# Reading the expert tiles in a circle that the token blocks join one by one, and comparing both keys in one VectorE operation for three of four tables

## The chip, the cores and the metric

The kernel runs on one core of a Trainium2 chip. The metric is the device time of one launch in microseconds (us); the time of the kernel before is the median of three runs. The engines are named as in the profile: PE (TensorE matmul; PEld its weight loads), DVE (VectorE), ACT (ScalarE), POOL (GpSimd) and SP (SyncE). SP issues plain DMAs, POOL issues gathers (indirect DMAs).

## What is computed

One layer of a transformer over 128 context tokens and 512 latent tokens of width 1024: adaptive norms, retention heads and neighbourhood attention, an output projection, and then PEER, a retrieval over 16384 single-neuron experts. The change is in PEER alone. For a block of 128 tokens, cut from the reference:

```
v1, i1 = top_k(s1, 16);  v2, i2 = top_k(s2, 16)        # 8 heads, two sets of 128 keys
top, sel = top_k(v1[:, None] + v2[None, :], 16)         # 16 of 256 pairs
eidx = i1 * 128 + i2  (of sel);   gate = softmax(top)
act = gelu(einsum('nd,nhkd->nhk', xb, u[eidx]))
y   = einsum('nhk,nhkd->nd', gate * act, v[eidx])
```

Each token has 128 chosen experts (8 heads of 16). `u` and `v` have 16384 rows of 1024 floats. There are five blocks of 128 tokens.

## The kernel before, in words

**Two ways through PEER.** For all five blocks, the rows of `u` are gathered: 128 gathers a block, each of 128 rows of 4 KB, one chosen expert for every token. DVE takes the dot product of each gathered tile with the block's input (a SCALAR_TENSOR_TENSOR of 128x1024). The fifth block, block 4, gathers its rows of `v` in the same way and adds them up in PSUM. Blocks 0 to 3 instead read all of `v`: they build a table W of weights, token by expert, and multiply it with `v`, read as 128 tiles of 128 rows (512 KB each). Tile i holds the experts with first key i.

**The tables.** `Dense.build(b)` (line 1571) builds the table of block b in 64 pairs of tokens. For a token it makes two one-hot matrices over the token's 128 chosen experts: one of the first key, scaled by the weight, and one of the second key. Their product, on PE, is the token's 128x128 table, second key by first key. For a pair m, DVE compares a row of numbers with the first keys (line 1600, bf16 result `eq`) and with the second keys (line 1601, fp32 result `B_`); ACT scales `eq` into `A_`, once for each token (line 1606); PE multiplies (two tokens); and every second pair ACT copies four tokens' tables from PSUM to `W` (line 1608). `eqs` and `oneh` have two buffers each, used in turn; `tabs`, which hold the keys and weights of the block, are one set.

There is room for two tables, `W[0]` and `W[1]`. Blocks 0 and 1 are group g = 0, blocks 2 and 3 group g = 1; block b uses `W[b % 2]`. Group 0 lays the table out so that the product's step i uses the memory rows i, and group 1 lays it out turned, so that token n lies in row n. So a token's table of block 2 can be written as soon as step n of block 0's product is done; each product needs its whole table.

**The products.** `product(0)` (line 1620) reads tile by tile of v and does four 128x512 matmuls with each, two for block 0 and two for block 1, in four PSUM banks. `product(1)` does the same for blocks 2 and 3. The last five tiles of the first round are kept and used first in the second (`NKEEP`), so v is read 251 times. `Stream` (line 444) holds the tiles of v in flight: a quota of six of the six tiles of the ring. `self.at` counts the steps done, and `build` of group 1 waits for it (line 1597). At the end of a product, `finish` (line 1551) closes a block in four pieces of 256 columns through one ring tile, halves of it in turn; `finish_with` (line 1543) closes a block from tiles loaded before.

**What sets the order.** The functions above are generators that record operations; `main` and `gathers` are interleaved by a count of PE and DMA time. `build(0)` is recorded beside the last key scores (line 1325); then `dense` (line 1678) records `build(1)`, then `product(0)` beside `build(2)` and `build(3)` (these two with PSUM banks 4 and 5 only), then `product(1)`. A planner (class `Plan`, from line 111) then orders all operations by their data, their priority and prices of its own (`cost`, lines 192 to 215), several times over, and emits the order that it finds shortest. Each engine runs its instructions in that order. Everything recorded passes line 365, so the profile names that line for all; the tile names tell the groups apart: `w` is the ring (and v), `arena` holds tables, gather tiles and the rest, `iota` marks the tables' compares. The gathers use tiles of their own (`gslots`, two at first, eight or nine late in the span).

Of the kernel before, what the change touches and what calls it, by code (L numbers as in the profile page):

```python
# [29 lines left out]
ROUNDS = ((0,), (1, 2, 3))  # L30
AHEADU = 1
XTRA = 3
NKEEP = 5


def bcast_rows(ap, n, width, offset=0):
# [332 lines left out]
def layer(ctx: ExitStack, tc: tile.TileContext, a: dict):  # L369
# [46 lines left out]
    def within(lo, hi, g):  # L416

        while True:
            old, banks[:] = list(banks), (lo, hi)
            r = next(g, "end")  # L420
            banks[:] = old
            if r == "end":
                return
            yield r

    def mm(out, lhsT, rhs, start, stop):
        nc.tensor.matmul(out, lhsT=lhsT, rhs=rhs, start=start, stop=stop)
        k, m = lhsT.shape[0], int(np.prod(lhsT.shape[1:]))
        n = int(np.prod(rhs.shape[1:]))
        up = lambda v: 32 if v <= 32 else 64 if v <= 64 else 128  # L430
        clk["PE"] += 4 * n / 2400.0 * up(k) / 128 * up(m) / 128
# [64 lines left out]
            ar.free(*lent.pop(id(t)))  # L496
            slots[:] = [x for x in slots if x is not t]

    S, SB, SV = Stream(NRING), Stream(2), Stream(NRING)

    def add_w(name, r, j, w, keep=None):
        for qt in range(4):
# [42 lines left out]
    for bl in ROUNDS:  # L545
        for h in range(8):
            lo, hi = 6 - 2 * bl[-1], 14 - 2 * bl[0]
            SB.add(("bias", bl, h), a["bias"][:, h, lo:hi, :], [hi - lo, 64])
    for t in list(range(P)) + list(range(P - NKEEP)):
        SV.add(("v", t), a["v"][P * t:P * t + P], [D])  # L550


    tc.nc.scalar.preload_act_table_set("natural_log_exp_and_others")
# [2 lines left out]
    def reserve():  # L556

        all_ = ar.alloc([19, P], lo=0, hi=12 * 256 // UNIT).ap
        oneh[:] = [all_[:, 4 * i:4 * i + 4].rearrange("s (z n) i -> s z n i", z=2) for i in range(2)]
        eqs[:] = [all_[:, 8 + i].bitcast(BF16).rearrange("s (i n) -> s i n", n=2) for i in range(2)]  # L560
        tabs[:] = [all_[:, 12], all_[:, 13], all_[:, 14].bitcast(BF16).rearrange("s (z n) -> s z n", z=2)]
        scb[:] = [all_[:, 15:19]]
        spare[:] = [all_[:, 0:8].rearrange("s a b -> s (a b)")]
# [974 lines left out]
    def prefetch(b, g, x):  # L1538
        if g is not None:
            nc.sync.dma_start(g, g2d[0 if b == 0 else 1])  # L1540
        nc.sync.dma_start(x, xres[b])

    def finish_with(b, acc, g, x):

        for j in range(2):
            col = slice(512 * j, 512 * j + 512)
            nc.vector.tensor_mul(acc[j], acc[j], g[:, col])
            nc.vector.tensor_add(x[:, col], x[:, col], acc[j])
            nc.sync.dma_start(a["y"][P * b:P * b + P, col], x[:, col])

    def finish(b, acc, t):

        for j in range(4):
            col = slice(256 * j, 256 * j + 256)
            g, x = (t[:, 512 * (j % 2) + 256 * z:512 * (j % 2) + 256 * z + 256] for z in range(2))
            nc.sync.dma_start(g, g2d[0 if b == 0 else 1][:, col])
            nc.sync.dma_start(x, xres[b][:, col])
            nc.vector.tensor_mul(g, acc[j // 2][:, 256 * (j % 2):256 * (j % 2) + 256], g)
            nc.vector.tensor_add(x, x, g)
            nc.sync.dma_start(a["y"][P * b:P * b + P, col], x)  # L1560
# [4 lines left out]
    class Dense:  # L1565
        def __init__(self):
            self.W = [None, None]
            self.at = P
            self.vkeep = {}

        def build(self, b):

            g, q = divmod(b, 2)
            if self.W[q] is None:
                self.W[q] = ar.alloc([P, P], top=True)
            Wn = self.W[q].ap
            if g == 0:
                Wn = Wn.rearrange("j i n -> j n i")
            while (b, 3) not in cready:
                yield "wait"  # L1580

            bt = bank()
            tr(bt.ap[:, 0:P], cw[b].rearrange("q h k -> q (h k)"))
            cT, ti, keys = tabs
            tii = ti.bitcast(I32)
            id_ = idx[b].rearrange("q h k -> q (h k)")
            for z, (op, s) in enumerate(((OP.arith_shift_right, 7), (OP.bitwise_and, 127))):
                nc.vector.tensor_single_scalar(tii, id_, s, op=op)
                nc.vector.tensor_scalar(ti, tii, 1.0, None, op0=OP.mult)
                tr(bt.ap[:, P * (z + 1):P * (z + 2)], ti)  # L1590
            nc.scalar.copy(cT, bt.ap[:, 0:P])
            nc.scalar.copy(keys, bt.ap[:, P:3 * P].rearrange("s (z n) -> s z n", z=2))
            ps.free(bt)
            full = None
            for m in range(P // 2):
                n0 = 2 * m
                while g == 1 and self.at < min(n0 + 4, P) and n0 % 4 == 0:
                    yield "at"
                eq, A_, B_ = eqs[m % 2], oneh[m % 2][:, 0], oneh[m % 2][:, 1]
                nc.vector.tensor_tensor(eq, iota2, keys[:, 0, None, n0:n0 + 2].to_broadcast([P, P, 2]), op=OP.is_equal)  # L1600
                nc.vector.tensor_tensor(B_, iota2.rearrange("s i n -> s n i"),
                                        keys[:, 1, n0:n0 + 2, None].to_broadcast([P, 2, P]), op=OP.is_equal)
                if n0 % 4 == 0:
                    bw = bank()
                for k in range(2):
                    nc.scalar.activation(A_[:, k], eq[:, :, k], AF.Copy, scale=cT[:, n0 + k:n0 + k + 1])
                if full is not None:
                    nc.scalar.copy(*full)
                    ps.free(last)
                    full = None  # L1610
                for k in range(2):
                    z = n0 % 4 + k
                    mm(bw.ap[:, P * z:P * z + P], B_[:, k], A_[:, k], True, True)
                if n0 % 4:
                    full, last = (Wn[:, n0 - 2:n0 + 2, :], bw.ap.rearrange("j (n i) -> j n i", n=4)), bw
                    yield
            nc.scalar.copy(*full)
            ps.free(last)

        def product(self, g):  # L1620
            acc = [[ps.alloc([512], hi=4) for _ in range(2)] for _ in range(2)]
            order = range(P) if g == 0 else list(range(P - NKEEP, P)) + list(range(P - NKEEP))
            for n, i in enumerate(order):
                if i not in self.vkeep:
                    v = SV.get(("v", i))
                else:
                    v = self.vkeep.pop(i)
                for q in range(2):
                    w = self.W[q].ap[:, i, :] if g == 0 else self.W[q].ap[:, :, i]
                    for j in range(2):  # L1630
                        mm(acc[q][j].ap, w, v[:, 512 * j:512 * j + 512], n == 0, n == P - 1)
                if g == 0 and i >= P - NKEEP:
                    self.vkeep[i] = v
                elif g == 0 and i == P - NKEEP - 1:
                    free = SV.held.pop(0)
                else:
                    SV.done()
                self.at = n + 1
                if g == 1 and n == P - 3:
                    last = [slots.pop() for _ in range(3)]  # L1640
                    prefetch(2, last[0], last[1])
                    prefetch(3, None, last[2])
                if n % 2:
                    yield
            while g == 1 and "v4" not in done:
                yield "wait"
            nc.gate = mark[0] if g == 1 else None
            for q in range(2):
                if g == 0:
                    finish(q, [x.ap for x in acc[q]], free)  # L1650
                    if q == 1:
                        slots.append(free)
                        SV.pump()
                else:
                    finish_with(2 + q, [x.ap for x in acc[q]], last[0], last[1 + q])
                ps.free(*acc[q])

    def both(*work):

        live = list(work)  # L1660
        while live:
            w = 0
            for z in list(live):
                r = next(z, "end")
                if r == "end":
                    live.remove(z)
                elif r is not None:
                    w += 1
                else:
                    yield  # L1670
            if live and w == len(live):
                yield "wait"

    def chain(*work):
        for w in work:
            yield from w

    def dense(dn):
        yield from dn.build(1)
        dn.at = 0  # L1680
        yield from both(dn.product(0), within(4, 6, chain(dn.build(2), dn.build(3))))
        yield from dn.product(1)


    def main():
# [127 lines left out]
```

## Time and profile before

| | us |
|---|---|
| three runs: median (lowest to highest) | 1906.23 (1904.07 to 1906.36) |
| the profiled execution, its own time | 1904.95 |
| its span, first to last instruction | 1903.1 |
| PE busy | 1777.2 (93%) |
| DVE busy | 1467.7 (77%) |
| ACT busy | 532.2 (28%) |
| POOL busy | 834.4 (44%) |

DMA moved 658.22 MB, a mean of 346 GB/s; 402.70 MB of it on POOL's queue (the gathers), 254.16 MB on SP's. The granted clock of PE was 0.958 of full speed on average.

How to read it: busy shares are averages over stages in which different resources are full, so the page's slices of 1/40 of the span and windows of chosen stretches say more. PE's busy time is of pipelined matmuls. A group's row has its count, busy time, mean, and the idle time of the engine just before its instructions with what ended it. A 128x512 fp32 matmul shows as two rows, so a tile of v for two blocks is eight.

### The profile page before, as it was taken

How to read it: one execution, taken by the hardware profiler on the slowest of the kernel's cores; microseconds unless marked ns; L12 is line 12 of the kernel's file. 1: busy time of each engine (PE TensorE's matmuls, PEld its weight loads, DVE VectorE, ACT ScalarE, POOL GpSimd, SP SyncE). 2: the span in 40 equal slices, each digit the busy share in tenths (PEclk: the TensorE clock that was granted, in tenths of full speed). 3: DMA queues.
4: the chain of work that ended last, by engine and by line, in shares of the span. 5: the costliest groups of instructions: out<-in, count | busy, mean ns of one | idle time of the engine just before them, and what ended most of it. 6: DMA issues, size and time to landing. Idle time of an engine off the chain costs nothing.

```text
span 1903.1 us, 21175 instructions
## 1 busy us (share of the span) xinstructions
PE 1777.2 (93%) x6096; PEld 1063.2 (56%) x6096; DVE 1467.7 (77%) x3785; ACT 532.2 (28%) x1368; POOL 834.4 (44%) x779
## 2 busy tenths in 40 slices
PE   7999999999999889867999999899987999999997
PEld 2438454455965466555444444355665666666665
DVE  2246998786879999999999996777998566666666
ACT  1225320133434334698211110122674000000000
POOL 0000467542137666524555544444435344444442
PEclk9998999999979889977999999899997999999999
DMA  9997889988759999857999999999978999999998
GB/s 363 316 327 246 313 278 339 393 311 307 271 178 344 365 336 378 317 177 210 364 408 401 392 408 409 387 409 406 358 242 275 410 409 409 409 409 409 409 409 330
DMA packets 203693, 658.22 MB, mean 346 GB/s; under 512 B 22572, under 2 KB 25900, under 8 KB 203448
## 3 DMA queue, kind: packets, MB, share of 16 engines
q0 software_dynamic: 110592, 402.70, 56.7%
q1 hardware_dynamic: 92984, 254.16, 35.5%
q8 instruction: 49, 0.80, 0.2%
q14 instruction: 68, 0.56, 0.1%
HBM read 645.51 MB, written 11.27 MB: 345 GB/s over the span
## 4 chain that ended last, share of the span: by engine, by line
DMA 27%; DVE 18%; PE 12%; issue 6%; ACT 2%; POOL 1%; DVEq 0%; POOLq 0%; ACTq 0%
DMA arena<-in_u,idx 15%; PE psum L365 12%; DMA arena<-in_v,idx 12%; DVE arena L365 12%; ACT arena L365 2%; DVE psum L365 1%; POOL arena L365 1%; DVE i L365 1%; DVE oh L365 1%; DVE vi L365 1%; DVE cand L365 0%; DVE idx L365 0%; DVE pi L365 0%; DMA w<-xres 0%; DMA out_y<-w 0%
## 5 line engine op out<-in xcount | busy, mean ns | idle before, releaser
L365 PE MATMUL psum<-w,arena 128*128 128x512 f32 (+1 forms) x2548 | 1094.2, 600 | 17.4 <-DVE arena L365 6.5
L365 POOL DMA_INDIRECT arena<-in_u,idx x640 | 711.6, 1112 | 899.8 <-DVE arena L365 486.6
L365 PEld LDWEIGHTS psum<-w,arena 128*128 128x128 f32 (+1 forms) x2548 | 560.4, 229 | 456.3 <-issue 280.2
L365 PE MATMUL psum<-arena 128*128 128x128 f32 (+5 forms) x2532 | 543.4, 366 | 65.3 <-ACT arena L365 34.1
L365 PEld LDWEIGHTS psum<-arena 128*128 128x128 f32 (+2 forms) x2532 | 374.3, 206 | 273.8 <-issue 137.3
L365 DVE SCALAR_TENSOR_TENSOR arena<-arena 128x1024 f32<-128x1024 f32 (+5 forms) x451 | 488.7, 1091 | 27.6 <-DMA arena<-in_u,idx 25.0
L365 DVE SCALAR_TENSOR_TENSOR arena<-arena,psum 128x1024 f32<-128x1024 f32 x256 | 308.4, 1214 | 92.6 <-DMA arena<-in_u,idx 92.6
L365 ACT ACTIVATE arena<-arena 128x128 f32<-128x128 bf16 (+7 forms) x626 | 237.7, 433 | 224.4 <-PE psum L365 103.8
L365 ACT COPY arena<-psum 128x512 f32<-128x512 f32 (+3 forms) x360 | 204.0, 581 | 316.6 <-PE psum L365 287.0
L365 DVE SCALAR_TENSOR_TENSOR psum<-arena,cw,psum 128x1024 f32<-128x1024 f32 x127 | 163.7, 1289 | 96.1 <-DMA arena<-in_v,idx 96.0
L365 DVE TENSOR_TENSOR arena<-iota,arena 128x256 f32<-128x256 bf16 (+1 forms) x512 | 160.7, 355 | 36.1 <-PE psum L365 33.3
L365 POOL DMA_INDIRECT arena<-in_v,idx x128 | 119.9, 937 | 141.5 <-DVE psum L365 118.1
L365 PE MATMUL psum<-arena,w 128*128 128x128 f32 (+1 forms) x640 | 132.0, 365 | 1.6 <-ACT arena L365 1.6
L365 PEld LDWEIGHTS psum<-arena,w 128*128 128x128 f32 x640 | 92.9, 196 | 31.4 <-ACT arena L365 2.3
L365 PE MATMUL psum<-ident,arena 128*128 128x128 f32 x372 | 64.9, 302 | 30.6 <-DVE arena L365 28.1
L365 PEld LDWEIGHTS psum<-ident,arena 128*128 128x128 f32 x372 | 48.7, 157 | 66.2 <-DVE arena L365 32.4
L365 DVE TENSOR_TENSOR arena<-arena 128x256 f32<-128x256 f32 (+6 forms) x131 | 61.0, 497 | 6.6 <-ACT arena L365 3.7
L365 ACT ACTIVATE zz<-dots 128x64 f32<-128x64 f32 x10 | 2.6, 255 | 196.3 <-DVE arena L365 196.3
L365 DVE TENSOR_TENSOR arena<-psum,arena 128x512 f32<-128x512 f32 (+1 forms) x40 | 27.1, 688 | 35.8 <-PE psum L365 34.7
L365 DVE TENSOR_REDUCE arena<-arena 128x8 f32<-128x512 f32 (+1 forms) x17 | 12.6, 743 | 46.2 <-ACT arena L365 46.2
L365 ACT ACTIVATE arena<-psum,arena 128x128 f32<-128x128 f32 (+2 forms) x102 | 34.7, 429 | 31.8 <-PE psum L365 27.6
L365 DVE MAX8 vi<-arena 128x8 f32<-128x128 f32 x128 | 30.0, 279 | 11.0 <-ACT arena L365 11.0
(74 smaller groups left out, 498.8 us busy)
## 6 DMA issues: line engine op xcount, KB each, us to landing
w<-in_v SPq DMA_DIRECT2D x251, 512.0 KB, 6.8
w<-in_w_ada SPq DMA_DIRECT2D x41, 512.0 KB, 5.4
w<-in_wq SPq DMA_DIRECT2D x40, 512.0 KB, 5.7
w<-in_w_in SPq DMA_DIRECT2D x36, 512.0 KB, 10.3
arena<-in_u,idx POOLq DMA_INDIRECT x640, 8.0
arena<-in_w_in SPq DMA_DIRECT2D x16, 512.0 KB, 9.4
w<-in_w_out SPq DMA_DIRECT2D x16, 512.0 KB, 5.7
arena<-in_x SPq DMA_DIRECT2D x9, 512.0 KB, 6.8
```

Source lines behind the costliest of these rows:

```text
L365: getattr(getattr(self.nc, eng), fn)(*args, **kw)
```

## The change

Tiles of v are read in a circle: step t reads tile t mod 128, for t from 0 to 283. Block 0 takes the steps 0 to 127, block 1 the steps 24 to 151 (it joins 24 steps later and so begins with tile 24), block 2 the steps 132 to 259 and block 3 the steps 156 to 283. A block joins only after its table is built. So steps 0 to 23, 128 to 131, 152 to 155 and 260 to 283 serve one block, the others two. The kept tiles go; the quota of v is five of the six ring tiles, and `finish` takes the sixth. Blocks 0, 1 and 2 end by `finish`, each at its own last step; block 3 alone ends by `finish_with` after block 4. `build(1)` is recorded beside the product, with `build(2)` and `build(3)` behind it, all with PSUM banks 4 and 5. Block 3's table is built in the order of block 1's steps, beginning with token 24.

In the tables of blocks 0, 1 and 2, one DVE operation of 512 elements compares both keys into bf16, and ACT copies the second key's half into fp32 `B_`. The fourth table, block 3's, keeps the two compares.

```diff
-NKEEP = 5
+JOIN = 24
+SETTLE = 4
...
-    S, SB, SV = Stream(NRING), Stream(2), Stream(NRING)
+    S, SB, SV = Stream(NRING), Stream(2), Stream(NRING - 1)
...
-    for t in list(range(P)) + list(range(P - NKEEP)):
-        SV.add(("v", t), a["v"][P * t:P * t + P], [D])
+    for t in range(2 * P + JOIN + SETTLE):
+        i = t % P
+        SV.add(("v", t), a["v"][P * i:P * i + P], [D])
...
-        eqs[:] = [all_[:, 8 + i].bitcast(BF16).rearrange("s (i n) -> s i n", n=2) for i in range(2)]
+        eqs[:] = [all_[:, 8 + 2 * i:10 + 2 * i].rearrange("s a b -> s (a b)").bitcast(BF16)
+                  .rearrange("s (z i n) -> s z i n", z=2, n=2) for i in range(2)]
...
-                while g == 1 and self.at < min(n0 + 4, P) and n0 % 4 == 0:
+                while g == 1 and self.at[q] < 2 * m + 4 and m % 2 == 0:
                     yield "at"
+                n0 = (2 * m + JOIN * (g * q)) % P
...
+                if b == 3:
+                    nc.vector.tensor_tensor(eq[:, 0], iota2, keys[:, 0, None, n0:n0 + 2].to_broadcast([P, P, 2]),
+                                            op=OP.is_equal)
+                    nc.vector.tensor_tensor(B_, iota2.rearrange("s i n -> s n i"),
+                                            keys[:, 1, n0:n0 + 2, None].to_broadcast([P, 2, P]), op=OP.is_equal)
+                else:
+                    nc.vector.tensor_tensor(eq, iota2[:, None].to_broadcast([P, 2, P, 2]),
+                                            keys[:, :, None, n0:n0 + 2].to_broadcast([P, 2, P, 2]), op=OP.is_equal)
+                    nc.scalar.copy(B_, eq[:, 1].rearrange("s i n -> s n i"))
...
+        def product(self):
+
+            begin = (0, JOIN, P + SETTLE, P + JOIN + SETTLE)
+            acc, total = {}, begin[3] + P
+            for t in range(total):
+                v, i = SV.get(("v", t)), t % P
+                for b in range(4):
+                    n = t - begin[b]
+                    if not 0 <= n < P:
+                        continue
+                    if n == 0:
+                        while b not in self.built:
+                            yield "wait"
+                        acc[b] = [ps.alloc([512], hi=4) for _ in range(2)]
+                    w = self.W[b % 2].ap[:, i, :] if b < 2 else self.W[b % 2].ap[:, :, i]
                     for j in range(2):
+                        mm(acc[b][j].ap, w, v[:, 512 * j:512 * j + 512], n == 0, n == P - 1)
+                    if b < 2:
+                        self.at[b] += 1
+                SV.done()
+                if t == total - 3:
+                    last = [slots.pop() for _ in range(2)]
+                    prefetch(3, *last)
+                for b in range(3):
+                    if t - begin[b] == P - 1:
+                        free = slots.pop()
+                        finish(b, [x.ap for x in acc[b]], free)
...
-        yield from dn.build(1)
-        dn.at = 0
-        yield from both(dn.product(0), within(4, 6, chain(dn.build(2), dn.build(3))))
-        yield from dn.product(1)
+        yield from both(dn.product(), within(4, 6, chain(dn.build(1), dn.build(2), dn.build(3))))
```

## Rows read from the trace of the kernel before

**Rows 1.** The page, part 2: forty equal slices of the span.

```profile
DVE  2246998786879999999999996777998566666666
GB/s 363 316 327 246 313 278 339 393 311 307 271 178 344 365 336 378 317 177 210 364 408 401 392 408 409 387 409 406 358 242 275 410 409 409 409 409 409 409 409 330
```

**Rows 2.** Stages: window, length, busy (x) of PE, PEld, DVE, ACT, POOL; clock, DMA, GB/s.

```profile
775.00:912.00 137.00, 100.11 (x495) 79.37 (x493) 130.61 (x372) 119.06 (x287) 56.77 (x53) 0.83 0.70 224
775.00:934.00 159.00, 121.62 (x546) 88.78 (x545) 152.61 (x467) 122.59 (x297) 69.46 (x64) 0.85 0.74 243
1325.00:1475.00 150.00, 128.71 (x558) 88.89 (x557) 139.94 (x352) 90.25 (x250) 67.04 (x69) 0.91 0.86 297
1475.00:1890.00 415.00, 415.00 (x968) 285.61 (x968) 255.07 (x283) 2.42 (x8) 180.76 (x193) 1.00 1.03 409
```

**Rows 3.** The chain of waits in order of time, late stretch: start, us, what.

```profile
...
1742.71 14.66 DMA arena<-in_v,idx
...
```

**Rows 4.** The page, part 6: reads of tiles of v.

```profile
w<-in_v SPq DMA_DIRECT2D x251, 512.0 KB, 6.8
```

**Rows 5.** Groups by form, 775 to 912 us: count | busy us, mean ns | idle before.

```profile
L365 ACT ACTIVATE arena<-arena 128x128 f32<-128x128 bf16 x216 | 70.1, 395 | 7.3 <-DVE arena L365 4.1 <-PE psum L365 3.1
L365 ACT COPY arena<-psum 128x512 f32<-128x512 f32 x56 | 57.1, 1031 | 7.6 <-PE psum L365 7.3
L365 PE MATMUL psum<-w,arena 128*128 128x512 f32 x17 | 8.3, 593 | 0.0
```

**Rows 6.** Timeline of ACT, then of DVE, 859 to 868 us.

```profile
859.47 1.04 ACT L365 COPY arena<-psum 128x512 f32<-128x512 f32 x1
862.00 1.04 ACT L365 COPY arena<-psum 128x512 f32<-128x512 f32 x1 [0.43 <-PE psum L365]
...
861.48 1.21 DVE L365 TENSOR_TENSOR arena<-iota,arena 128x256 f32<-128x256 bf16 x4
862.61 1.21 DVE L365 SCALAR_TENSOR_TENSOR arena<-arena 128x1024 f32<-128x1024 f32 x1
```

**Rows 7.** Groups by form, whole span: compares on DVE, plain ACT work.

```profile
L365 DVE TENSOR_TENSOR arena<-iota,arena 128x256 f32<-128x256 bf16 x256 | 105.6, 419 | 34.3 <-PE psum L365 33.3
L365 DVE TENSOR_TENSOR arena<-iota,arena 128x256 bf16<-128x256 bf16 x256 | 70.5, 291 | 1.8 <-ACT arena L365 1.4
L365 DVE TENSOR_TENSOR oh<-oh,i 128x1600 bf16<-128x1600 bf16 x20 | 19.7, 984 | 3.6 <-ACT oh L365 3.6
L365 ACT COPY arena<-psum 128x128 f32<-128x128 f32 x88 | 23.0, 268 | 42.9 <-PE psum L365 42.5
L365 ACT ACTIVATE arena<-arena 128x512 f32<-128x512 f32 x25 | 15.8, 631 | 8.4 <-DVE arena L365 8.1
```

**Rows 8.** Timeline of SP, then of DVE, 1395 to 1442 us.

```profile
1395.13 1.04 SPq L365 DMA_DIRECT2D w<-g2d  x2
...
1441.79 28.38 SPq L365 DMA_DIRECT2D w<-in_v  x5
...
1417.90 0.42 DVE L365 TENSOR_TENSOR w<-psum,w 128x256 f32<-128x256 f32 x1
```

**Rows 9.** Stages of 25 us where the fourth table ends.

```profile
1400.00:1425.00 25.00, 17.54 (x99) 14.00 (x98) 22.55 (x65) 18.91 (x54) 7.79 (x8) 0.96 0.72 218
1425.00:1450.00 25.00, 15.36 (x60) 12.73 (x60) 24.38 (x63) 15.09 (x41) 11.55 (x12) 0.57 0.81 258
1450.00:1475.00 25.00, 20.82 (x65) 14.74 (x66) 19.67 (x39) 6.34 (x16) 13.71 (x15) 0.92 0.82 288
```

**Rows 10.** Timeline of DVE at the end.

```profile
1895.20 1.29 DVE L365 TENSOR_TENSOR psum<-psum,w 128x512 f32<-128x512 f32 x2
```

**Rows 11.** Timeline of PE where the third table begins.

```profile
1215.04 0.48 PE L365 MATMUL psum<-ident,arena 128*128 128x128 f32 x1 [9.31 <-DVE arena L365]
```

**Rows 12.** DMA issues, 1475 to 1890 us: count, us to landing.

```profile
w<-in_v SPq DMA_DIRECT2D x116, 512.0 KB, 6.8
arena<-in_v,idx POOLq DMA_INDIRECT x128, 14.6
```

More of the change, by code (lines that the diff above doesn't have):

```diff
@@ L1567, in __init__ @@
             self.W = [None, None]
-            self.at = P
-            self.vkeep = {}
+            self.at = [0, 0]
+            self.built = set()
         def build(self, b):
@@ L1595, in build @@
             for m in range(P // 2):
-                n0 = 2 * m
-                while g == 1 and self.at < min(n0 + 4, P) and n0 % 4 == 0:
+                while g == 1 and self.at[q] < 2 * m + 4 and m % 2 == 0:
                     yield "at"
+                n0 = (2 * m + JOIN * (g * q)) % P
                 eq, A_, B_ = eqs[m % 2], oneh[m % 2][:, 0], oneh[m % 2][:, 1]
-                nc.vector.tensor_tensor(eq, iota2, keys[:, 0, None, n0:n0 + 2].to_broadcast([P, P, 2]), op=OP.is_equal)
-                nc.vector.tensor_tensor(B_, iota2.rearrange("s i n -> s n i"),
-                                        keys[:, 1, n0:n0 + 2, None].to_broadcast([P, 2, P]), op=OP.is_equal)
+                if b == 3:
[7 more added lines that the diff above has]
+                    nc.scalar.copy(B_, eq[:, 1].rearrange("s i n -> s n i"))
                 if n0 % 4 == 0:
@@ L1605, in build @@
                 for k in range(2):
-                    nc.scalar.activation(A_[:, k], eq[:, :, k], AF.Copy, scale=cT[:, n0 + k:n0 + k + 1])
+                    nc.scalar.activation(A_[:, k], eq[:, 0, :, k], AF.Copy, scale=cT[:, n0 + k:n0 + k + 1])
                 if full is not None:
@@ L1618, in build @@
             ps.free(last)
[L1620 to L1629, printed above, removed]
-                    for j in range(2):
[L1631 to L1651, printed above, removed]
@@ new lines, in build @@
+            self.built.add(b)
+        def product(self):
[12 more added lines that the diff above has]
+                    w = self.W[b % 2].ap[:, i, :] if b < 2 else self.W[b % 2].ap[:, :, i]
+                    for j in range(2):
+                        mm(acc[b][j].ap, w, v[:, 512 * j:512 * j + 512], n == 0, n == P - 1)
[9 more added lines that the diff above has]
+                        finish(b, [x.ap for x in acc[b]], free)
@@ L1652, in product @@
                         slots.append(free)
                         SV.pump()
-                else:
-                    finish_with(2 + q, [x.ap for x in acc[q]], last[0], last[1 + q])
-                ps.free(*acc[q])
+                        ps.free(*acc[b])
+                if t % 2:
+                    yield
+            while "v4" not in done:
+                yield "wait"
+            nc.gate = mark[0]
+            finish_with(3, [x.ap for x in acc[3]], *last)
+            ps.free(*acc[3])
```

## The prediction, before the result was known

> **What bounds the kernel now.** I read the page's slices first, to find where the engines change places, then the windows by stage, then the chain of waits, and last the groups by form and timelines of the stages that the change touches. In the slices DVE stands at nine tenths through the middle, and the DMA rate at about 409 GB/s from slice 20 on, with two dents: slices 17 and 18, and 29 and 30 [rows 1]. The windows say what the dents are [rows 2]. From 775 to 912 us the first two tables are built: DVE is busy 130.6 of 137 us, ACT 119.1, and DMA moves only 224 GB/s. From 1325 to 1475 us the fourth is built while v is hardly read: 297 GB/s. From 1475 to 1890 us PE has no idle time at all and DMA is full at 409 GB/s, and the chain at the end goes from one gather to the next, each landing about 14.7 us after its issue [rows 3]. So two resources end last together: DMA, which must move a fixed number of bytes, and PE, which must make the products. A change pays only by the bytes and matmuls it moves into the two dents, less what it adds. The forecast is two sums, one for each, and the later one counts.
>
> Units: one tile of v or one gather is 0.524 MB, 1.28 us at 409 GB/s. 968 matmul rows in 415 us are 0.429 us each [rows 2]; a tile for one block is four such rows, 1.71 us, and for two blocks 3.43 us.
>
> **Added reading.** 251 reads of v [rows 4] become 2·128+24+4 = 284: 33 more, +42.3 us of DMA. SP's issuing is idle most of the time there; the count on SP costs nothing. Bounds: nothing, if all of them fall into idle DMA, to 42.3. I book the whole here and the filling of the dents below.
>
> **First dent (tables 0 and 1).** 216 activations make 108 pairs of tokens in 137 us [rows 5]. ACT's strided copies start 2.54 us apart for two pairs, with 0.43 us of waiting for PE in them, and DVE is full with four compares and one dot in the same time [rows 6]. What changes for a pair:
> - DVE: 419+291 ns go [rows 7]. The one compare over 512 two-byte elements is not shown; between 291 ns for 256 and 984 ns for 1600 the line gives 0.42 us (bounds 0.29, and 0.71 for no gain). About 0.29 us saved a pair, in three tables of four.
> - ACT: a cast of 128x256 is added. Bounds 268 ns (128 elements) and 631 ns (512) [rows 7]; the line gives 0.39, and since activations that read the same tile take 395 against 268 ns, I take 0.42. ACT then needs 2.54+0.84, less the 0.43 of waiting that the casts fill: 2.95 us for two pairs. So ACT paces the stage, and it ends 54·0.41 = 22 us later, at 934 (+6 to +68 us by the bounds, the upper one with the wait kept).
>
> In return block 0's product runs alone under table 1: 24 tiles, and a ring of five behind them, some 27 reads within the window. The gathers go with the dots that DVE finds time for. Today 53 go out [rows 2], one for two pairs. The order of instructions is the planner's; by its own prices (lines 192 to 215, used for the order, not for time) DVE has room for 1.41 dots for two pairs when ACT paces, 76 in all. I take 70. So the stage moves 97 transfers, 50.9 MB, where the same 159 us now move 243·159 = 38.6 MB [rows 2]: 12.3 MB ahead, −30 us. Bounds: gathers stay at 53, −8 us; DMA full, 65.0 MB, −65 us.
>
> PE: block 0's 24 tiles are 41 us. Now PE has by 934 done 17 rows before 912 (7 us) [rows 5] and 22 us after: 29. −12 us.
>
> [...]
>
> **Second dent (table 3).** Now two blocks end together: their ends begin at 1395 with two loads, the second half is read from PSUM at 1417.9, and SP issues no read of v until 1441.8 [rows 8], since kept tiles hold the ring. After the change blocks 0 and 1 end 24 steps apart, v goes on, and table 3 trails block 1's product. Those 28 steps are 8 single and 20 double, 82 us of PE; 64 pairs of four rows of 128 columns, a quarter of 0.429 us each, make 110, and two waits (below) 132. DVE is busy 93% of today's stage [rows 2]. Of 123 us, table 3 takes 36, as its four compares for two pairs take 1.13 us from start to the next start [rows 6], and two block ends, 16 operations at 0.42 us [rows 8], take 7. The rest is 66 dots at 1.21 us [rows 6]. With 28 tiles that is 94 transfers, 120 us of 132; 12 us lost where now (409−297)·150 = 16.8 MB, 41 us, are lost [rows 2]. I take −29 us (0 to −41).
>
> PE's own loss there is 21.3 us idle and about 9 us at the lower clock (granted 0.57 in the middle stretch) [rows 9]: −30 us. Against it stand two new waits, at steps 132 and 156. The new block needs the old one's second PSUM bank, freed 22.8 us after its end began [rows 8]; four single steps cover 6.8 us, the ring's next tiles for the other block up to 8.5, earlier loads some more. I take what lies between 7.5 and 16 us, 11 each: +22 us (0 to 32).
>
> **The end.** One block rather than two is closed after the gate; four of DVE's half-row operations, twice 1.29 us [rows 10], go: −2.6 us.
>
> **Sums.** The profiled execution took 1904.95 us (span 1903.1 and 1.9 around it), 1.3 below the median of 1906.23. DMA: 1904.95+42.3−30−29−2.6 = 1885.7, with 1.3 added 1887. PE: 1906.2−12−30+22−2.6 = 1883.6; PE also stands 9.3 us where table 2 begins, behind DVE [rows 11], and table 3 now begins within the products too; half of that again gives 1888. The two agree within their errors; the later, **1888 us**, is the forecast. Where the stalls go, DMA is late next.
>
> **Rivals.**
> 1. Both dents fill entirely. DMA: 1904.95+42.3−65−41−2.6+1.3 = 1840; PE with covered waits: 1906.2−12−30−2.6 = **1862**, and PE bounds. For it: gslots and POOL have room, POOL is busy 57 of 137 us [rows 2]. Against: DVE is nearly full in both dents. Chance 0.17.
> 2. ACT paces the tables and the gathers gain nothing, because the fixed order still gives one dot for two pairs and DVE waits for its two compare buffers with dots queued behind. Then the first dent gives 8 us, and the second, DVE-bound as now, 12: 1904.95+42.3−8−12−2.6+1.3 = **1926**. It decides once the dents give back less than about 41 us together. For it: ACT busy 119 of 137 us before a cast is added [rows 2]. Against: 27 reads of v need no DVE. Chance 0.26. [...]
> 3. Block 3 is alone in the last 24 steps and wants a tile each 1.71 us, 0.75 of the DMA rate. If gathers take half, a tile comes each 2.56 us: 24·0.85 = 20 us, **1908**. Against: in the full stage a read of v lands in 6.8 us, a gather in 14.6 [rows 12], and five in flight make one each 1.36 us. The Trainium skill, "DMA: Bandwidth & Descriptors" (Queues, rings and completion order), says that each engine goes round-robin over queues at packet granularity, which would be that half; the trace's 6.8 us speaks for more than half. Chance 0.12.
> 4. The change doesn't do what it says: the replanned order puts table 1 ahead of block 0's product, the 24 single steps come after the dent, and PE loses 41−29+22 more: about 1930. Chance 0.04.
>
> **How the numbers follow.** The forecast has 0.41 (1875 to 1902, its two sums' errors). About 0.2% (3.8 us) is what a measurement of this kernel can tell from no change. Faster: the forecast's case, rival 1 and a little of the others, 0.60. Same (1902.4 to 1910.0): most of rival 3 and some of 2, 0.11. Slower: 0.29. The range goes from 1860, just under rival 1, to 1926, rival 2's time; about 0.09 lies on either side. The forecast's own range is 1875 to 1902.
>
> **What would show it.** Right: 284 reads of v; DMA above 300 GB/s while tables 0 and 1 are built, matmuls of products beginning before 850 us, ACT the engine that paces there (copies some 2.95 us apart) and DVE with idle time; no gap of 40 us in the reads of v; a 128x512 compare at 0.42 us and casts near 0.42. Wrong: DMA near 224 GB/s in the first dent, or PE waiting over 15 us for PSUM at the block changes, or DMA not full in the last 40 us while PE waits for v.

## The result, and the profile after

The changed kernel takes **1913.39 us** (median of 10 runs, 1907.91 to 1920.09), beside 1902.62 for the kernel before on the same chip (10 runs). The ratio is 1.0059, 95% interval 1.0039 to 1.0079: slower by 0.6%, where 1.0% faster was forecast. The time lies within the range of 1860 to 1926; the sign is wrong. The profiled execution took 1913.24 us, its span 1911.5, which is 8.4 us more than the span of before. Runs over 1.5% above the fastest of the same kernel count as slow and are left out of its ratio; this befell experiment 11 alone, with seven of its 12 runs, the profiled one among them.

I read the page first. The lines are PE and the DMA rate over forty slices of the span, then the reads of v from its part 6.

```profile
PE   7989998999999889879999999899699899999987
GB/s 364 313 333 265 300 270 346 390 308 290 275 227 331 322 357 387 358 268 403 343 408 409 408 409 409 381 410 382 343 410 352 372 409 409 409 409 409 409 351 198
...
w<-in_v SPq DMA_DIRECT2D x284, 512.0 KB, 6.8
```

The 284 reads are there, and both dents of [rows 1] are shallower. But DMA now runs empty at the end (351, then 198 GB/s, where before it held 409, then 330), while PE stands at eight tenths in the last slice but one, where before it held nine. The same in windows (columns as in [rows 2]):

```profile
775.00:912.00 137.00, 114.93 (x490) 80.63 (x489) 126.99 (x327) 126.05 (x336) 67.89 (x66) 0.83 0.93 339
775.00:934.00 159.00, 135.50 (x579) 93.30 (x578) 147.54 (x383) 148.05 (x398) 78.79 (x76) 0.85 0.94 344
1325.00:1475.00 150.00, 128.16 (x464) 85.06 (x463) 125.36 (x288) 67.28 (x191) 70.31 (x74) 0.87 0.98 372
1850.00:1875.00 25.00, 12.97 (x26) 7.48 (x25) 3.23 (x8) 0.00 (x0) 0.00 (x0) 0.73 0.64 208
```

Where tables 0 and 1 are built, DMA moves 339 GB/s (224 before); where table 3 is built, 372 (297 before). So the two dents were filled, and the time didn't come. The groups by form, of the whole span, have the prices of the new operations:

```profile
L366 DVE TENSOR_TENSOR arena<-iota,arena 128x512 bf16<-128x512 bf16 x192 | 79.8, 423 | 32.1 <-ACT arena L366 30.7
...
L366 ACT CAST arena<-arena 128x256 f32<-128x256 bf16 x192 | 80.3, 418 | 22.3 <-DVE arena L366 21.5
```

**Where PE's lead went.** The products are 2048 rows on PE in both kernels, so counting those done by a given time shows who leads. This is the windows view of the tile `w` on PE alone, each window from 840 us on: length, PE busy and (x) rows done, clock, DMA. First before, then after.

```profile
840.00:1200.00 360.00, 294.56 (x682) 0.97 0.95 361
840.00:1500.00 660.00, 503.73 (x1135) 0.96 0.94 356
840.00:1844.00 1004.00, 847.73 (x1937) 0.97 0.97 374
```

```profile
840.00:1200.00 360.00, 315.97 (x714) 0.99 1.00 392
840.00:1500.00 660.00, 520.81 (x1139) 0.95 0.99 384
840.00:1844.00 1004.00, 864.81 (x1940) 0.97 1.00 393
```

At 1200 us the new kernel leads by 32 rows, 13.7 us at 0.429 us a row. At 1500 us 4 rows are left of that: 12 us were lost while one pair of blocks followed the other. From 1500 to 1844 nothing changes. Then, with 108 rows to go (46.3 us), the products should end at 1890.3; they end at 1904.8. PE's timeline from 1840 us, before and after:

```profile
1839.59 52.52 PE L365 MATMUL psum<-w,arena 128*128 128x512 f32 x122
```

```profile
1839.76 18.19 PE L366 MATMUL psum<-w,arena 128*128 128x512 f32 x42
1869.97 34.80 PE L366 MATMUL psum<-w,arena 128*128 128x512 f32 x76 [12.03 <-DMA w<-in_v]
```

PE stands 12.03 us for a tile of v although the last gather has been used up 48 us earlier than before (DVE's last multiply-add on one begins at 1843.66, before at 1891.48). The chain of waits says what it stands for (start, us, what; the short pieces between are left out):

```profile
1848.54 3.60 DMA w<-g2d
...
1853.17 2.79 DMA out_y<-w
...
1856.02 6.68 DMA w<-xres
...
1863.69 2.55 DMA out_y<-w
...
1866.32 3.52 DMA w<-in_v
...
1869.97 31.38 PE psum L366 x68
```

This is the closing of block 2: `finish` loads the gate and residual into a ring tile, multiplies, adds and stores, four pieces in turn. Then `slots.append(free)` gives that tile back to the ring, and the next read of v that gets it can be issued only when the last store has landed. The Trainium skill, "DMA: Bandwidth & Descriptors" (Two DMAs through the same engine are not ordered), says that the issuing engine has to wait on the first DMA's semaphore before a dependent one. The trace agrees: the last store starts at 1863.69 and takes 2.55 us, and the read follows at 1866.32.

PE needs that one tile. The 76 rows behind its wait are 19 steps of block 3, and SP issues only 14 reads from 1866.32 on, so the tiles of five later steps lie in the ring already; from 1870 to 1874 us DMA moves nothing. PE takes the steps in their order, and stands for the first. SP's timeline, then the window (columns as in [rows 2]):

```profile
1866.32 28.52 SPq L366 DMA_DIRECT2D w<-in_v  x14
```

```profile
1870.00:1874.00 4.00, 4.00 (x5) 1.78 (x6) 0.00 (x0) 0.00 (x0) 0.00 (x0) 0.51 0.00 0
```

From 1320 us on the same happens with block 0's tile. SP's timeline there:

```profile
1351.34 0.33 SPq L366 DMA_DIRECT2D w<-in_v  x1
1357.81 0.81 SPq L366 DMA_DIRECT2D out_y<-w  x2
1363.44 90.96 SPq L366 DMA_DIRECT2D w<-in_v  x19
```

and PE's, where product rows are `psum<-w,arena`:

```profile
1349.23 2.08 PE L366 MATMUL psum<-w,arena 128*128 128x512 f32 x2 [3.43 <-DVE w L366]
...
1373.74 1.91 PE L366 MATMUL psum<-w,arena 128*128 128x512 f32 x2
```

After one read at 1351.34 none is issued until the closing's last stores have landed, and PE's next product rows begin at 1373.74. In between PE has only matmuls of table 3, at which it waits for DVE five times, 11.3 us together. DMA shows the hole only in part, since gathers go on: it moves 245 GB/s from 1351 to 1363 us.

### The profile page after: what moved, and what is told of

Its sections match the earlier page's. It is cut to its first block, busy times and chain, and to the rows that moved or that the text cites. A ratio compares the mean times of both kernels' runs of the same rounds, so it can differ in the third digit from the quotient of the medians.

```text
span 1911.5 us, 20947 instructions
## 1 busy us (share of the span) xinstructions
PE 1782.6 (93%) x6096; PEld 1062.3 (56%) x6096; DVE 1428.2 (75%) x3597; ACT 582.0 (30%) x1560; POOL 824.5 (43%) x779
## 4 chain that ended last, share of the span: by engine, by line
PE 30%; DVE 14%; DMA 14%; ACT 5%; issue 3%; POOL 1%; DVEq 0%; SPq 0%; ACTq 0%; POOLq 0%
PE psum L366 30%; DMA arena<-in_u,idx 11%; DVE arena L366 10%; ACT arena L366 4%; DMA w<-g2d 1%; DVE i L366 1%; POOL arena L366 1%; DVE vi L366 1%; DVE oh L366 1%; DMA w<-in_v 1%; DMA out_y<-w 1%; DVE cand L366 0%; DMA arena<-in_x 0%; DVE pi L366 0%; DMA w<-xres 0%
## 5 line engine op out<-in xcount | busy, mean ns | idle before, releaser
L366 PE MATMUL psum<-w,arena 128*128 128x512 f32 (+1 forms) x2548 | 1110.0, 604 | 33.1 <-DMA w<-in_v 15.0
L366 POOL DMA_INDIRECT arena<-in_u,idx x640 | 701.7, 1096 | 860.3 <-DVE arena L366 425.8
L366 PE MATMUL psum<-arena 128*128 128x128 f32 (+5 forms) x2532 | 545.7, 367 | 55.6 <-DVE arena L366 25.8
L366 PEld LDWEIGHTS psum<-arena 128*128 128x128 f32 (+2 forms) x2532 | 378.5, 205 | 289.7 <-issue 158.2
L366 DVE SCALAR_TENSOR_TENSOR arena<-arena 128x1024 f32<-128x1024 f32 (+6 forms) x451 | 489.3, 1093 | 24.7 <-DMA arena<-in_u,idx 23.6
L366 ACT ACTIVATE arena<-arena 128x128 f32<-128x128 bf16 (+7 forms) x626 | 257.9, 448 | 219.0 <-PE psum L366 98.2
L366 DVE TENSOR_TENSOR arena<-iota,arena 128x512 bf16<-128x512 bf16 (+2 forms) x320 | 119.6, 396 | 34.6 <-ACT arena L366 30.7
L366 ACT CAST arena<-arena 128x256 f32<-128x256 bf16 x192 | 80.3, 418 | 22.3 <-DVE arena L366 21.5
```

What stands on the lines that cost most here:

```text
L366: getattr(getattr(self.nc, eng), fn)(*args, **kw)
```

## The experiments

Three theories stood: **P** (products on PE end last, and PE loses its time where one block follows another), **B** (33 more reads on a full DMA are the cost), **A** (the casts make ACT pace the tables). Ratios are to the kernel before on the same chip. The chips differed: its median lay between 1902.5 and 1923.0 us, so times of different batches compare by ratio.

**1. The changed kernel with 33 gathers fewer.** It leaves out 33 of block 4's 128 experts, as many bytes as the added reads.

```diff
-        seq += [("v", 4, s) for s in range(P)] + [("g2", 4, 0), ("x", 4, 0)]
+        seq += [("v", 4, s) for s in range(P - 33)] + [("g2", 4, 0), ("x", 4, 0)]
```

> The changed kernel with 33 of block 4's 128 gathers of v left out: block 4's output lacks those 33 experts. It takes away as many bytes as the change added reads of v (17.3 MB, 42 us of full DMA). Theory P (the products on PE end last; PE loses its time where one block follows another): the time stays within 6 us of the changed kernel's 1913, and the last gather lands some 40 us before 1843. Theory B (the 33 added reads on a full DMA are the cost): 30 to 42 us faster, 1871 to 1883.

Measured 1908.64 us, 1.0037 (1.0007 to 1.0066): 4.8 us below the changed kernel by medians, 4 by ratio, with intervals that overlap. The gathers' last use falls from 1843.7 to 1800.6 us, and PE still stands 10.60 us for v, at 1864.82. B falls for the changed kernel: 43 us of earlier DMA are worth some 5.

**2. The same edit in the kernel before.** The same 33 experts are left out.

> The kernel before with 33 of block 4's 128 gathers of v left out; block 4's output lacks those experts. Theory P says PE was the last resource in the kernel before too, as its products end 0.6 us after the last gather: 0 to 10 us faster than 1902. Theory B says DMA was the bound of before: 30 to 42 us faster.

Measured 1876.22 us, 0.9867 (0.984 to 0.9893): 29 us faster, and P's 0 to 10 missed. So the same bytes, with the sums on DVE that go with them, cost 29 us before the change and 5 after it. PE's products end earlier too: 1996 rows are done at 1844 us, 59 more than in the kernel before, which is 25 us of work (how much of that the new order does isn't known). So P is wrong for the kernel before, where PE's end hung on DMA and DVE; in the changed kernel it does so far less.

**3. The circle without the casts.** All four tables keep two compares.

```diff
-                if b == 3:
+                if True:
```

> The circle alone: all four tables with the two compares of before, no casts. Theory A (the casts make ACT pace tables 0 to 2, and that costs): tables 0 and 1 end about 22 us earlier than in the changed kernel, and the time falls by 8 to 20 us to 1893 to 1905. Theory P: tables 0 and 1 end earlier, but DVE is full again, fewer gathers go out in that stage, and the waits at the block changes stay: within 8 us of 1913, either way.

Measured 1929.98 us (4 runs, 1923.97 to 1931.18), 1.0114 (1.0079 to 1.0149): by ratio 10 us, by medians 17 us slower than the changed kernel. A falls, since without casts it is worse. P's bound of 8 us was missed too. DVE is full in the first stage:

```profile
775.00:850.00 75.00, 65.57 (x310) 47.39 (x308) 74.40 (x211) 54.41 (x131) 48.91 (x35) 0.93 0.88 327
```

At 1200 us 667 product rows are done, 47 fewer than with casts, and PE then stands 25.8 us for v from 1200 us on (15.0 with casts). How much of the loss is DVE's and how much the new order's isn't told apart.

**4. The casts without the circle.** The kernel before, with one compare and the cast in tables 0 to 2.

```diff
...
+                    nc.vector.tensor_tensor(eq, iota2[:, None].to_broadcast([P, 2, P, 2]),
+                                            keys[:, :, None, n0:n0 + 2].to_broadcast([P, 2, P, 2]), op=OP.is_equal)
+                    nc.scalar.copy(B_, eq[:, 1].rearrange("s i n -> s n i"))
...
```

> The kernel before with the change's one compare and cast for tables 0 to 2 and nothing else. Theory A: slower by 10 to 25 us (1913 to 1928), as table 1 is built alone and ends some 20 us later, with the products behind it. Theory P: the casts lengthen the stage before the products start, so it is slower too, by 10 to 20 us; what tells the theories apart is that here the cast has no product beside it. If it is within 4 us of 1903, the casts cost nothing in either kernel.

Measured 1909.99 us, 1.0034 (1.0012 to 1.0056): 6.5 us slower, less than expected. In its windows ACT is full and DMA nearly idle where the first product waits for its tables:

```profile
900.00:925.00 25.00, 20.39 (x70) 14.45 (x68) 22.84 (x78) 24.97 (x64) 1.18 (x2) 0.59 0.12 43
```

So the cast alone costs 6.5 us, while the circle is 10 to 17 us worse without it (experiment 3). That block 0's product covers the longer table stage there would explain both; no run tests that by itself.

**5. Block 2 closed at the end.** Its closing moves behind the products and goes through two gather tiles; only blocks 0 and 1 return a ring tile.

```diff
-                for b in range(3):
+                for b in range(2):
...
+            two = [gslots.pop(0) for _ in range(2)]
+            prefetch(2, *two)
...
+            finish_with(2, [x.ap for x in acc[2]], *two)
...
```

> The changed kernel, but block 2 is closed at the end through two tiles of the gathers, which are free by then, and not through the sixth ring tile between the reads of v. Theory P: PE's wait of 12.0 us for v at 1858 to 1870 goes, and most of the cold clock behind it; the product ends 12 to 18 us earlier, and the time is 1896 to 1903. Theories A and B: within 4 us of 1913.

Measured 1890.35 us (5 runs), **0.9923** (0.9888 to 0.9959): faster than both kernels, and by more than P expected. PE has no wait in the end; its timeline there is one piece, through to 1882:

```profile
1839.76 42.22 PE L366 MATMUL psum<-w,arena 128*128 128x512 f32 x98
```

It also has 20 rows more at 1500 us than the changed kernel (1159 against 1139), 8.6 us that the edit doesn't explain by itself: the planner made another order.

**6. Experiment 5 with SETTLE = 10**, six more single steps between the pairs of blocks.

> As the run that closes block 2 late (1890), with SETTLE = 10 for 4: ten single steps between blocks rather than four, six more reads of v. If PE's waits at the block changes come from the table that ends too late and from the old block's bank, six more steps of 1.71 us cover up to 10 us at each of the two changes: 1872 to 1885. If PE's order is what costs there (table rows placed ahead of product rows and waiting for DVE), it stays within 6 us of 1890.

Measured 1901.82 us, 0.9986 (0.9966 to 1.0005), some 11 us above experiment 5. Neither expectation held, and more cover didn't help: PE's waits for DVE and ACT grew from 26.2 to 33.9 us from 1200 us on.

**7. Experiment 5 with short closings.** Blocks 0 and 1 are stored as they are; gate and residual are left out.

```diff
-            nc.sync.dma_start(g, g2d[0 if b == 0 else 1][:, col])
-            nc.sync.dma_start(x, xres[b][:, col])
-            nc.vector.tensor_mul(g, acc[j // 2][:, 256 * (j % 2):256 * (j % 2) + 256], g)
-            nc.vector.tensor_add(x, x, g)
+            nc.vector.tensor_copy(x, acc[j // 2][:, 256 * (j % 2):256 * (j % 2) + 256])
```

> As the run that closes block 2 late, and blocks 0 and 1 close without loads: the gate and the residual of those blocks are left out, the sum is copied from PSUM and stored. If the chain of load, multiply, store through one ring tile holds PE at the block changes, the waits there (PSUM bank, reads of v behind stores on SP) go: 1875 to 1885. If it is the tables' pace, it stays within 5 us of 1890.

Measured 1878.51 us (4 runs), 0.9874 (0.985 to 0.9897), by medians 12 us and by ratios 9 us less than experiment 5. At 1500 us 1193 rows are done, 34 more, 14.6 us. So the chain in the closings does hold PE between the pairs of blocks. By which of its parts isn't told apart, since loads and DVE work go together: PE's waits for DVE and ACT from 1200 us on fall from 26.2 to 14.6 us, those for v stay (3.3 and 3.9).

**8. Experiment 5 in another order**: the planner's price for the landing of an SP load goes from 1.0 to 5.0 us. It changes no operation, only the order.

> As the run that closes block 2 late, and the planner believes that an SP transfer lands 5 us after the bus and not 1 us. No work changes, the order alone. If the planner's belief in early loads puts stores and table rows ahead of product rows, the waits shrink: 1875 to 1886. If not, within 6 us of 1890, either way: that is also the size of what a new order alone does.

Measured 1940.86 us, 1.0199 (1.0177 to 1.0222): 50 us more than experiment 5, with one wait of 18.1 us for v. Neither expectation held. This is the caution on every run here: an edit also gets a new order, and an order alone can move this kernel by 2.7%. So a theory needs its waits in the trace beside its time.

**9. A tile of its own for the closings.** The changed kernel, but the sixth ring tile is taken once, and never given back to the circle; v's quota is five tiles in both.

```diff
+            free = slots.pop()
             for t in range(total):
...
-                        free = slots.pop()
                         finish(b, [x.ap for x in acc[b]], free)
-                        slots.append(free)
-                        SV.pump()
```

> The changed kernel, and the sixth ring tile is kept for closings and never goes back into the circle. Theory P in its narrower form (a read of v into the tile that a closing has just used waits for the closing's last store, and the products wait for that read): the waits of PE at 1353 to 1374, 1491 to 1494 and 1858 to 1870 go, 12 to 28 us, and the time is 1885 to 1901, with the closings still between the reads. If stores on SP hold all reads behind them, whatever the tile, the wait near 1858 stays above 6 us and the time is within 6 us of 1913.

Measured 1906.96 us beside 1923.01 for before on this chip: **0.9929** (0.9901 to 0.9957), faster than both kernels. All closings and their stores are still issued on SP between the reads, so it isn't their being there. The reads of v now go on between the pieces of a closing, as SP's timeline shows (the stores are block 0's, the loads of `g2d` already block 1's):

```profile
1380.35 0.34 SPq L366 DMA_DIRECT2D out_y<-w  x1
1380.74 0.43 SPq L366 DMA_DIRECT2D w<-g2d  x1
1381.58 3.77 SPq L366 DMA_DIRECT2D w<-in_v  x2
1385.44 0.38 SPq L366 DMA_DIRECT2D out_y<-w  x1
1385.87 0.42 SPq L366 DMA_DIRECT2D w<-g2d  x1
1388.44 2.27 SPq L366 DMA_DIRECT2D w<-in_v  x2
```

The own tile does a second thing with it: half of a closing's loads come long before the closing (block 1's first stores are issued at 1479.72), so its chain is shorter too. This run doesn't tell the two apart.

**10. The changed kernel once more**, on a chip like that (before 1919.66 us), as experiment 9's control.

> The changed kernel once more, unaltered, beside the next run on one chip, so that the two can be compared directly. P: ratio to the kernel before between 1.003 and 1.009, as in the result, and a wait of 10 to 13 us for a tile of v in the last 70 us. If the order or the chip made the difference instead, the ratio lies within 0.002 of 1.

Measured 1935.27 us, 1.0086 (1.0053 to 1.0118), with the wait at the end at 11.62 us. PE's waits from 1200 us on, in this run (waited for, us in total, times, longest):

```profile
PE psum L366 <- DVE arena L366: 22.5, 9, 6.0
PE psum L366 <- DMA w<-in_v: 12.1, 2, 11.6
PE psum L366 <- issue: 6.6, 2, 6.0
PE psum L366 <- ACT arena L366: 6.0, 7, 1.6
PE psum L366 <- DVE w L366: 3.5, 1, 3.5
```

and with a tile of its own for the closings:

```profile
PE psum L366 <- DMA w<-in_v: 3.4, 3, 2.6
PE psum L366 <- issue: 0.9, 2, 0.5
```

50.7 us against 4.3. A part of this is order: experiment 9 builds table 2 earlier, and its waits there fall before 1200 us. From 775 us on, with both orders' waits for the tables counted in, the sums are 73.9 and 43.3 us; the difference is 30.6 us, and the two ratios give 30. The waits for DVE that go are 16.6 us at matmuls of table 3, and 5.9 at the head of table 2. That PE stands at table 3 only because no tile of v is there to work on is likely, and not shown.

The profiled runs lie further apart, as one is among the slower ones here (1945.95 us) and the other the fastest of experiment 9 (1896.51). Rows done say where the gain lies (the view of tile `w`, as above; this run, then experiment 9):

```profile
840.00:1325.00 485.00, 399.68 (x894) 0.95 0.99 383
840.00:1600.00 760.00, 592.79 (x1297) 0.94 0.99 383
```

```profile
840.00:1325.00 485.00, 394.29 (x874) 0.95 1.00 389
840.00:1600.00 760.00, 632.88 (x1389) 0.97 1.00 389
```

Experiment 9 is 20 rows behind before the first closing and 92 ahead after the second. From 1325 to 1500 us, this run and then experiment 9 (columns as in [rows 2]):

```profile
1325.00:1500.00 175.00, 154.37 (x588) 101.67 (x586) 150.27 (x338) 91.56 (x263) 83.67 (x87) 0.90 0.99 379
```

```profile
1325.00:1500.00 175.00, 174.53 (x716) 116.79 (x715) 153.18 (x356) 106.55 (x307) 78.74 (x83) 1.00 0.99 379
```

At the same 379 GB/s PE is busy 20 us longer, and at the full clock.

**11. Only block 2 keeps its tile.**

```diff
-                        slots.append(free)
-                        SV.pump()
+                        if b < 2:
+                            slots.append(free)
+                            SV.pump()
```

> Block 2's closing keeps its ring tile instead of giving it back; blocks 0 and 1 give theirs back as before, so that the two earlier changes of block stay and the end alone is altered. P (the tile that comes back is what PE waits for): the wait of 12 us in the last 70 us falls below 3 us, the half clock behind it goes too, and the time is 9 to 15 us below the changed kernel's on the same chip, so 0.997 to 1.001 of the kernel before. Rival (the closing's DMAs on SP's queue delay the reads, whichever tile they go to): the wait stays at 8 us or more and the time within 4 us of the changed kernel's. Second rival (the replanned order decides): the wait goes and the time moves by less than half of it, or the other way.

Measured 1.0038 (1.001 to 1.0066) from the five of 12 runs that count (1914.1 to 1937.5 us). Beside experiment 10 that is 9 us less, as P said. But the intervals overlap, the ratio lies above P's 0.997 to 1.001, and the median of all 12 runs is 1944.5 us, above experiment 10's, so the size isn't settled. In its profile the wait at the end is 2.07 us, where it was 11.62: the tile's return alone was taken away, with the chain of the closing as it was. What else that profile shows isn't used.

**12. Experiments 5 and 9 together.**

> Both: block 2 closed late through gather tiles, and the sixth ring tile kept for the closings of blocks 0 and 1. Theory P in its narrower form: the wait at 1353 to 1374 goes, some 10 us below the run that closes block 2 late alone, 1876 to 1886. If the first block change is held by table 2's end and by DVE and not by the tile: within 5 us of 1890.

Measured 0.9948 (0.9925 to 0.9972): no better than either alone. By ratio that is 1893 us on experiment 5's chip, so P's narrower form is missed and its rival's time (within 5 us of 1890) is met. The rival's reason isn't borne out by the trace, though. Beside experiment 9, on the same chip, 42 rows fewer are done at 1200 us (540 against 582) and 39 fewer at 1600 us (1350 against 1389): this order loses them ahead of the first closing, and nothing at the changes of blocks.

## Why the prediction was wrong, step by step

**The reading of before was right in part.** Both ends do lie together: DVE's last multiply-add on a gather begins at 1891.48 us, and the last product row ends at 1892.1. But they aren't two bounds side by side. Experiment 2 takes work from DMA and DVE alone; by the later of two sums it would have gained nothing, and it gained 29 us, 25 of them in PE's products by 1844 us. So PE's sum couldn't be made apart from DMA's.

**Prices and the first dent were right.** The compare of 512 elements took 423 ns (0.42 us taken), the cast 418 ns (0.42). ACT paces the stage: DVE is as busy (147.54 us from 775 to 934 us, ACT 148.05), but PE's waits from 775 to 1200 us are all for ACT, 23.1 us, and 46 strided copies fall in 125 us from 800 us on, 2.7 us apart (2.95 forecast). The stage moved 344 GB/s · 159 us = 54.7 MB (50.9 forecast, 38.6 before), 39 us of full DMA where 30 were forecast. PE gained 13.7 us (12 forecast).

**The sum for DMA was nearly right, but no longer set the end.** The second dent gave (372 − 297) · 150 = 11.3 MB, 27.5 us (29 forecast). At 1843.7 us the gathers were done, and 108 rows were left, 24 single steps and one and a half double ones. That is at most 26 tiles, 33 us of full DMA: DMA alone could have been done at 1877. That is 14 us earlier than the last gather of before; 19 was forecast. But the prediction then took the later of two sums as if each ran by itself. The gathers came out 48 us sooner, since they had the DMA time that the reads of v left; what remained was mostly block 3's single steps, at PE's pace.

**The step that failed is the sum for PE, at the changes of blocks and at the end.** For the second dent it has −30 us, two waits for a PSUM bank of 11 us each, and 4.7 for the head of the third table: −3 in all. Measured: +12. The −30, PE's idle time and low clock there, didn't come: in the same window, 1325 to 1475 us, PE is idle 21.8 us (21.3 before) at a clock of 0.87 (0.91). The wait for the bank is there and small, 3.43 us. What decides, by experiments 7, 9 and 10, is the closing with its tile on its way back into the ring, which the prediction put at nothing.

It stood in the trace of before. [rows 8] was read as two ends that begin at 1395 us, with reads of v held off by kept tiles. The first loads are at 1378.13, and the sixth ring tile, which the kept tiles leave, is the closing's. SP's timeline of before:

```profile
1378.13 0.33 SPq L365 DMA_DIRECT2D w<-g2d  x1
...
1434.86 2.69 SPq L365 DMA_DIRECT2D out_y<-w  x2
```

The read at 1441.79 comes right behind: SP waits 4.2 us for a store `out_y<-w` before it. So the chain from the first load to the next read took 63.7 us for two blocks. The second bank, too, was free only after its last read, which begins at 1431.61, and not after 22.8 us.

For the end the sum for PE has −2.6 us. The fewer operations after the products gave more, 4.3 us (11.0 us from the products' end to the span's end before, 6.7 after), but the products lost 14 us, for which the sum has no term: 12.03 of waiting for the tile that block 2's closing gives back, and 2.2 since PE's granted clock is 0.51 for a while after it (76 rows take 34.80 us rather than 32.6). The sum by what was measured, −13.7 + 12 + 14 − 4, is +8, and the spans differ by 8.4. That the time still lies in the range is luck: its upper end is the second rival's time, which had another reason.

**The rivals.** The first had PE as the bound, which is right, with all waits covered, which isn't; experiment 9 comes nearest to that, with 4.3 us of waits from 1200 us on. The second had ACT full, which is right, and gathers that gain nothing, which isn't: 66 go out from 775 to 912 us, 53 before (its break-even of 41 us is 39.7 by its own terms). The third had PE short of v in the last 24 steps because gathers take half of DMA: PE was short there, but the gathers had long ended, so the sharing wasn't tested. The fourth didn't come: product rows begin at 849.33 us, and 103 are done by 934 (its 34 us above 1888 make 1922, not 1930). Of what would show the forecast wrong, "DMA not full in the last 40 us while PE waits for v" is what came, and what I had no mechanism for.

**What stays open**: why the circle without casts loses 10 to 17 us, which part of a closing holds PE between the pairs of blocks, and how much of each run is its new order.

## What to carry to other kernels

A buffer lent from a ring to a side job and given back puts that job's whole chain (load, multiply, add, store, landing) in front of one later read of the stream, and an engine that takes the stream in order stands for that one buffer, however many others lie loaded: keep such a buffer out of the circle, or move the side job behind the stream. When two resources end together, ask whether the end of one hangs on the other, and what each has left once the other is done, rather than take the later of two sums. Where a tool replans the order with each edit, change the order alone once, and trust a cause only where its wait is gone from the trace and hasn't moved to another stage.

## What the runs showed of the hardware

A load of 128 KB for a closing, issued at 1333.69 us under gathers and reads, had landed at 1348.76, when the DVE multiply that waited for it began, 15.1 us later; at the end, with the gathers gone, such a load took 3.6 us (1848.54). From its first load to the read into its tile, block 0's closing took 43.5 us (1319.91 to 1363.44), block 2's 17.8 (1848.54 to 1866.32). PE's granted clock was 0.50 of full speed, the lower of its two levels, from 1862 to 1869 us, while PE stood for v, 0.51 from 1870 to 1874, when it worked again, and 1.00 from 1874 to 1878, so that a wait of 12 us cost 14.
